# A two-layer hybrid decoder trunk in float32: the state's decay moved into keys and queries, two inverse roots queued later, and weight splits placed behind the first tile's transposed split

## The chip, the cores and the metric

The kernel runs on one core of a Trainium2 chip, in one launch. The metric is the time of one execution on the device in microseconds, as the median of several runs. The engines of the core are TensorE (PE, with its weight loads as PEld), VectorE (DVE), ScalarE (ACT), GpSimd (POOL) and SyncE (SP), which issues the transfers. Each engine works through its own queue of instructions in the order in which the program holds them; they wait for each other by semaphores.

## The reference

The input x is (1, 256, 1024) in float32. Two layers of three parts each follow: a half-step SwiGLU, a mixer, another half-step SwiGLU. Each part is normed on both sides.

```python
x = x + 0.5 * rmsnorm((silu(h @ w_gate) * (h @ w_up)) @ w_down, post_g)   # h = rmsnorm(x, pre_g)
x = x + rmsnorm(mixer(rmsnorm(x, pre_g)), post_g)
```

The mixer of layer 0 is a sparse attention beside a gated short convolution. The mixer of layer 1 is RWKV-7: for each of 16 heads a state of 64 by 64 runs over the 256 steps,

```python
def step(state, inp):
    r_t, w_t, k_t, v_t, kk_t, a_t = inp
    sa = jnp.einsum("bhij,bhj->bhi", state, -kk_t)
    state = (state * w_t[:, :, None, :] + sa[..., None] * (kk_t * a_t)[:, :, None, :]
             + v_t[..., None] * k_t[:, :, None, :])
    return state, jnp.einsum("bhij,bhj->bhi", state, r_t)
```

and its output is normed by head, given a bonus and a gate, and projected.

## The kernel before

Six stages run one after the other: `l0_ffn1`, `l0_mix`, `l0_ffn2`, `l1_ffn1`, `l1_mix`, `l1_ffn2`. The 256 rows of x are two tiles of 128 (`m` = 0 and 1). Every matmul with weights is made of three (`mm3`, lines 282 to 284): each operand is split into a high part that PE can take at its fast rate and a low remainder, and high by high, high by low and low by high are added up in PSUM. Weights come in transfers of up to 1 MB into one of four `raw` buffers; a piece of 1024 columns is split by `split_free`: ACT writes the high part (`L241`), DVE the remainder in one instruction or, for every `share`-th piece, POOL in two (`L246`).

**From one stage to the next.** The last part of a stage is `out_proj`: it finishes tile 0 first, then tile 1. `post_norm` takes the banks of a finished tile: ACT sums the squares (`L297`), ACT and POOL make the inverse root (`rstd`, `L290` and `L291`), DVE adds the result to x (`L356`). While PE works on tile 1, the next stage's `pre_norm` treats tile 0: squares, the product with the gain (`xg`, `L314`), the inverse root, and the scaling to `xn` (`L319`). `hT_split` has PE transpose `xn` (`L326`) and splits the result (`split`, ACT `L217`, DVE `L218`). PE's first matmuls of the next stage read both halves of it.

In the meantime the first weight pieces of the next stage are split too. `pre_norm` of tile 0 sets `self.held` to a list of instructions and `self.free` to 4. The first four pieces after it are free, and every later one is issued only after the instructions of that list (`split_u`). Before the change the list holds the latest square, product with the gain and inverse root.

Nothing here fixes the whole order by hand: a scheduler gives each engine its queue, under the data's order and these added constraints. So where an instruction stands has to be read from the built program.

**The RWKV chain.** The 256 steps are four chunks of 64 (`j` = 0 to 3). `kstep` prepares, for each of eight blocks of two heads (`c`), a tile `KR(c)` that holds for each chunk the scaled kappa and r side by side (columns 0 to 63 and 64 to 127), and `BK(c)` with the keys; `ff[:, c, j]` is the decay over chunk `j`. `gram` multiplies `BK` by `KR` (PE `L1145`). `chain(j)` then applies the state: `KR` times state into the banks `kb` (`L1338`), further terms (`L1342`), the scaled result `u` (DVE `L1344`), a small solve (`L1355`, copied by ACT in `L1356`), the chunk's contribution to the state into a bank `b` (`L1363`), the new state, and the output (`L1378`). For `j` = 1 and 2 the new state is decay times old state (POOL, `sf`) plus decay times `b` (DVE, `L1366` and `L1371`); for `j` = 0 there is no old state, and DVE multiplies `b` by the decay (`L1373`). `chunk_norm(j)` sums squares, makes an inverse root of 16 values for 64 rows (`L1403` to `L1408`, with ACT's square root `L1404` in between) and scales the output (`L1418`). `head_out(m)` applies gate and bonus (`L1428`, `L1429`) and has PE transpose the result for the last projection.

The string `TAIL` gives the order in which these generators are advanced (digits: `chain`; a to d: `chunk_norm(0)` to `(3)`, the first letter(s) sums, the next the root, then the scaling; p and q: `head_out`; o: the projection), and PE's instructions are kept in that order. `FILL` gives the order of work that fills the base solve ahead of it.

## Time and profile before

| | |
|---|---|
| time, median of 3 runs | 1160.28 us (1158.94 to 1164.31) |
| time of the profiled execution | 1160.69 us |
| its span, first to last instruction | 1159.0 us, mean granted TensorE clock 0.978 |
| busy: PE, DVE, ACT, POOL | 1093.6, 701.2, 601.0, 429.6 us (94, 61, 52, 37% of the span) |
| chain that ended last | 76% PE, 15% DVE, 4% issue, 3% ACT, 1% POOL |
| memory traffic | 185 MB read, 161 GB/s over the span |

The shares of busy time are means over stages. The 1.7 us between the time and the span lie around the first and the last instruction. Where a text names a time of day such as "at 197 us", it counts from the start of the span. A granted clock of 1.00 is PE's full rate.

### The profile page before, as it was taken

The numbers are of one execution on the slowest core, as the hardware profiler recorded it, in microseconds if no ns is written. First come the engines' busy times: TensorE is split into PE (matmuls) and PEld (weight loads), VectorE is DVE, ScalarE is ACT, GpSimd is POOL, SyncE is SP. The second block draws the span as 40 slices with busy tenths as digits, with TensorE's granted clock in tenths as the row PEclk, the third lists the DMA queues.
The fourth block names the chain that finished last, engine by engine and source line by source line (L and its number), as shares of the span: only waits on it lengthen the run. The fifth ranks groups of instructions, "written<-read, shape, count | busy, mean of one in ns | idle before, by whom it ended". The sixth has DMA issues, their size and how long they took to land.

```text
span 1159.0 us, 16840 instructions
## 1 busy us (share of the span) xinstructions
PE 1093.6 (94%) x6429; PEld 921.9 (80%) x6429; DVE 701.2 (61%) x1177; ACT 601.0 (52%) x1130; POOL 429.6 (37%) x390
## 2 busy tenths in 40 slices
...
GB/s 331 252 216 180 184 207 89 148 146 73 163 164 168 231 207 171 205 182 180 164 201 200 184 184 126 145 147 74 92 54 92 57 150 160 244 192 188 176 109 36
DMA packets 130749, 187.46 MB, mean 162 GB/s; under 512 B 6871, under 2 KB 101087, under 8 KB 130670
## 3 DMA queue, kind: packets, MB, share of 16 engines
...
HBM read 185.34 MB, written 1.05 MB: 161 GB/s over the span
## 4 chain that ended last, share of the span: by engine, by line
PE 76%; DVE 15%; issue 4%; ACT 3%; POOL 1%; DMA 0%; SPq 0%; DVEq 0%; POOLq 0%; ACTq 0%
PE mm L429 10%; PE fl L429 10%; PE fl L284 7%; PE fl L282 6%; PE fl L283 6%; PE fl L430 5%; PE mm L430 5%; PE mm L282 5%; PE mm L284 5%; PE mm L283 5%; DVE u L246 3%; PE tr L326 2%; PE fl L433 1%; PE mm L433 1%; DVE xn L1220 1%
## 5 line engine op out<-in xcount | busy, mean ns | idle before, releaser
L246 POOL TENSOR_TENSOR u<-raw,u 128x512 fp32r<-128x512 f32 x222 | 321.7, 1471 | 496.1 <-ACT u L241 490.4
L241 ACT ACTIVATE u<-raw 128x1024 fp32r<-128x1024 f32 x312 | 327.5, 1058 | 276.7 <-PE mm L283 78.5
L246 DVE TENSOR_TENSOR u<-raw,u 128x1024 fp32r<-128x1024 f32 x201 | 272.7, 1362 | 210.5 <-ACT u L241 210.2
L429 PE MATMUL mm<-b,u 128*128 128x512 f32 x504 | 181.3, 398 | 0.0
L429 PE MATMUL fl<-b,u 128*128 128x512 f32 x504 | 180.6, 397 | 0.0
L430 PE MATMUL fl<-b,u 128*128 128x256 f32 x504 | 141.5, 281 | 0.0
L430 PE MATMUL mm<-b,u 128*128 128x256 f32 x504 | 141.4, 281 | 0.0
L284 PE MATMUL fl<-u,b 128*128 128x512 f32 (+1 forms) x304 | 118.4, 390 | 3.5 <-DVE b L218 3.0
L282 PE MATMUL fl<-u,b 128*128 128x512 f32 (+1 forms) x304 | 118.7, 393 | 2.6 <-DVE u L800 1.3
L283 PE MATMUL fl<-u,b 128*128 128x512 f32 (+1 forms) x304 | 118.4, 389 | 1.5 <-DVE u L246 1.5
L282 PE MATMUL mm<-u,b 128*128 128x512 f32 (+1 forms) x296 | 114.7, 389 | 0.0
L283 PE MATMUL mm<-u,b 128*128 128x512 f32 (+1 forms) x296 | 113.0, 383 | 0.0
L284 PE MATMUL mm<-u,b 128*128 128x512 f32 (+1 forms) x296 | 112.5, 382 | 0.0
L429 PEld LDWEIGHTS mm<-b,u 128*128 128x128 f32 x504 | 94.8, 188 | 19.7
L429 PEld LDWEIGHTS fl<-b,u 128*128 128x128 f32 x504 | 94.9, 188 | 19.5
L430 PEld LDWEIGHTS mm<-b,u 128*128 128x128 f32 x504 | 95.2, 189 | 3.3
L430 PEld LDWEIGHTS fl<-b,u 128*128 128x128 f32 x504 | 95.2, 189 | 3.1
L284 PEld LDWEIGHTS fl<-u,b 128*128 128x128 f32 x304 | 57.8, 190 | 16.9 <-DVE b L218 4.3
L282 PEld LDWEIGHTS fl<-u,b 128*128 128x128 f32 x304 | 58.0, 191 | 15.1 <-ACT b L217 2.0
L283 PEld LDWEIGHTS fl<-u,b 128*128 128x128 f32 x304 | 58.0, 191 | 12.9 <-DVE u L246 1.7
L282 PEld LDWEIGHTS mm<-u,b 128*128 128x128 f32 (+1 forms) x296 | 55.8, 189 | 11.8 <-issue 0.7
L283 PEld LDWEIGHTS mm<-u,b 128*128 128x128 f32 (+1 forms) x296 | 55.9, 190 | 10.6
...
## 6 DMA issues: line engine op xcount, KB each, us to landing
...
```

The source lines that it names most:

```text
L241: self.nc.scalar.activation(hi, src, AF.Copy)
L246: (self.nc.gpsimd if pool else self.nc.vector).tensor_sub(lo[c], src[c], hi[c].bitcast(F32))
L282: mm(out, a[0], b[0], start=start, stop=False)
L283: mm(out, a[0], b[1], start=False, stop=False)
L284: mm(out, a[1], b[0], start=False, stop=stop)
L326: t = self.nc.tensor.transpose(pt[:, j * P:(j + 1) * P], src[:, j * P:(j + 1) * P], self.ident)
L429: mm(b2, w[k][0], x, start=k == 0, stop=False)
L430: mm(b2[:, 0], w[k][1], x[:, 0], start=False, stop=False)
L433: mm(b2, w[k][0], x, start=False, stop=True)
L1220: ins = [e.tensor_tensor(x, x, t, op=ALU.subtract) for e, x, _, _, t in act]
```

## The change

There are three parts.

1. **Decay.** New ACT copies (`decayed()`, 24 of 128 by 128) multiply chunk `j` of `KR(c)` by the decay of chunk `j` − 1, for `j` = 1 to 3. The state is kept without its last decay: for `j` = 1 and 2 DVE adds `b`, read from PSUM, to `sf`, and the four multiplications `L1366` are gone; `sf` uses the decay of chunk `j` − 1. For `j` = 0 the state is a plain copy of `b`, two quarters of it by DVE and two by ACT.
2. **TAIL.** The root of chunk 1 and that of chunk 2 are advanced later, and the transposed half of `head_out(0)` with them.
3. **Stage changes.** The list `held` of tile 0 now is the high and the low part of its transposed split and the inverse root (square, scaled x and inverse root where the stage takes its gain by columns), and none of the four free pieces goes to POOL. POOL's instructions for splits fall from 222 to 204, nine pieces; DVE's rise by nine.

```diff
-    FILL = "vvvz-vvtvvvbvvvhth-vvvvtthvtvtvv-h-vv-h-"
+    FILL = "vvvz-vvtvvvbvvvhthkvvvvtthvtvtvvkhkvvkh-"
-    TAIL = ("vvvgvz0xxvxx0A00gAggsB0eA000aAy1a1y1a1aa1yBy11b1bb2B22b2B2b222ocpocc33cc33p3d/3dooddodqooo"
+    TAIL = ("vvvgvz0xxvxx0A00gAggsB0eA000aAy1a1y1a1aa1yBy11b1b2B2b2b2B2b222ococ33cpcc33p3d/3dooddodqooo"
...
-                self.hT_split(self.pre_norm(m, g), hl, m)
+                hi, lo = self.hT_split(self.pre_norm(m, g), hl, m)
+                if m == 0:
+                    self.held[:2] = hi.ins, lo.ins
...
-        pool = self.share and self.nlo % self.share == 0
+        pool = self.share and self.nlo % self.share == 0 and self.free < 0
...
-                self.tail_of["xg"] = nc.vector.tensor_tensor(xg[:, sl], self.x[m][:, sl], g[:, sl], op=ALU.mult).ins
+                nc.vector.tensor_tensor(xg[:, sl], self.x[m][:, sl], g[:, sl], op=ALU.mult)
         r = self.rstd(ss)
+        for sl in self.HALF:
+            self.tail_of["xn"] = nc.vector.tensor_scalar(xn[:, sl], xg[:, sl], r, None, op0=ALU.mult).ins
         if m == 0 and g is not None:
-            self.held, self.free = list(self.tail_of.values()), 4
-        for sl in self.HALF:
-            nc.vector.tensor_scalar(xn[:, sl], xg[:, sl], r, None, op0=ALU.mult)
+            self.held, self.free = [self.tail_of[n] for n in ("sq", "xn", "pow")], 4
...
-            ffb = lambda ps, cs: ff[ps, cs, j:j + 1].to_broadcast([ps.stop - ps.start, cs.stop - cs.start, 64])
+            ffb = lambda ps, cs: ff[ps, cs, j - 1:j].to_broadcast([ps.stop - ps.start, cs.stop - cs.start, 64])
...
-                    if j:
-                        t = u[:, h * 512:h * 512 + 256].rearrange("p (c i) -> p c i", c=4)
-                        V.tensor_mul(t, b, ffb(slice(0, P), ch[h]))
...
-                            V.tensor_add(dst, sf[ps, ch[h]], t[ps])
+                            V.tensor_add(dst, b[ps], sf[ps, ch[h]])
+                        elif q:
+                            SC.activation(dst, b[ps], AF.Copy)
                         else:
-                            V.tensor_mul(dst, b[ps], ffb(ps, ch[h]))
+                            V.tensor_copy(dst, b[ps])
...
+        def decayed():
+
+            for c in range(NC):
+                for j in range(1, CH):
+                    SC.activation(KR(c)[:, j, :], KR(c)[:, j, :], AF.Copy, scale=ff[:, c, j - 1:j])
+                if c % 2:
+                    yield
```

Line numbers of the changed kernel are higher by 2 from line 216 on and by 3 from about line 353 on, up to `chain`: `L246` is `L248` there, `L291` is `L293`, `L326` is `L328`, `L356` is `L359`, `L1344` is `L1347`; in `chunk_norm` and `head_out` they are higher by 2 (`L1403` is `L1405`).

**Queues at the change into `l0_ffn2`.** POOL's queue there, before: the rows `L246` are the halves of weight pieces, `L291` the inverse roots, in order of tile 0's `post_norm` and `pre_norm` and the same two of tile 1.

```order
L246 TENSOR_TENSOR u<-raw,u 128x512 [waits PE_49,DMAHW3_49,Activation_49,Pool_49]
L246 TENSOR_TENSOR u<-raw,u 128x512
L246 TENSOR_TENSOR u<-raw,u 128x512 [waits DMAHW4_49,PE_49,Activation_49]
L246 TENSOR_TENSOR u<-raw,u 128x512
L291 TENSOR_TENSOR rstd_3124<-rstd,nhalf 128x1 [waits Activation_49]
L291 TENSOR_TENSOR rstd_3141<-rstd,nhalf 128x1 [waits Activation_49]
L246 TENSOR_TENSOR u<-raw,u 128x512 [waits DMAHW6_49,PE_49,Activation_49]
L246 TENSOR_TENSOR u<-raw,u 128x512
L291 TENSOR_TENSOR rstd_3220<-rstd,nhalf 128x1 [waits Activation_49]
```

POOL's queue at the same place after the change:

```order
L937 AFFINE_SELECT pk<-pk 64x64 [waits DVE_49,Pool_49]
L937 AFFINE_SELECT pk<-pk 64x64
L293 TENSOR_TENSOR rstd_3122<-rstd,nhalf 128x1 [waits Activation_49,Pool_49]
L293 TENSOR_TENSOR rstd_3139<-rstd,nhalf 128x1 [waits Activation_49]
L293 TENSOR_TENSOR rstd_3218<-rstd,nhalf 128x1 [waits Activation_49]
L248 TENSOR_TENSOR u<-raw,u 128x512 [waits DMAHW6_49,PE_49,Activation_49]
L248 TENSOR_TENSOR u<-raw,u 128x512
L293 TENSOR_TENSOR rstd_3235<-rstd,nhalf 128x1 [waits Activation_49]
L248 TENSOR_TENSOR u<-raw,u 128x512 [waits DVE_49,DMAHW0_49,PE_49,Activation_49]
```

The first two pieces have left POOL, and the first three inverse roots stand ahead of the splits. On DVE at the same place, before: `L314` is the product with the gain, `L319` the scaling, `L218` the low part of the transposed split.

```order
L314 TENSOR_TENSOR xn<-x_96,gain 128x512 [waits DVE_49] x2
L300 TENSOR_SCALAR sse<-ss 128x1 [waits Activation_49] x2
L353 TENSOR_TENSOR xn<-mm,gain 128x512
L246 TENSOR_TENSOR u<-raw,u 128x1024 [waits DMAHW5_49,PE_49,Activation_49]
L319 TENSOR_SCALAR xn<-xn,rstd_3141 128x512 [waits DVE_49,Pool_49]
L319 TENSOR_SCALAR xn<-xn,rstd_3141 128x512 [waits DVE_49]
L246 TENSOR_TENSOR u<-raw,u 128x1024 [waits PE_49,Activation_49]
L246 TENSOR_TENSOR u<-raw,u 128x1024 [waits DMAHW6_49,PE_49,Activation_49]
L218 TENSOR_TENSOR b_3018<-tr,b_3018 128x4x128 [waits Activation_49]
L218 TENSOR_TENSOR b_3019<-tr,b_3019 128x4x128 [waits Activation_49]
L246 TENSOR_TENSOR u<-raw,u 128x1024 [waits DMAHW7_49,PE_49,Activation_49]
```

And after:

```order
L248 TENSOR_TENSOR u<-raw,u 128x1024 [waits PE_49,Activation_49]
L356 TENSOR_TENSOR xn<-fl,gain 128x512 [waits Activation_49]
L359 SCALAR_TENSOR_TENSOR x_96<-xn,rstd_3122,x_96 128x512 [waits DVE_49,Pool_49]
L359 SCALAR_TENSOR_TENSOR x_96<-xn,rstd_3122,x_96 128x512 [waits DVE_49]
L316 TENSOR_TENSOR xn<-x_96,gain 128x512 [waits DVE_49] x2
L302 TENSOR_SCALAR sse<-ss 128x1 [waits Activation_49] x2
L356 TENSOR_TENSOR xn<-mm,gain 128x512
L319 TENSOR_SCALAR xn<-xn,rstd_3139 128x512 [waits DVE_49,Pool_49]
L319 TENSOR_SCALAR xn<-xn,rstd_3139 128x512 [waits DVE_49]
L220 TENSOR_TENSOR b_3016<-tr,b_3016 128x4x128 [waits Activation_49]
L220 TENSOR_TENSOR b_3017<-tr,b_3017 128x4x128 [waits Activation_49]
L248 TENSOR_TENSOR u<-raw,u 128x1024 [waits DMAHW5_49,Activation_49]
```

Between the product with the gain and the split's low part (`L220`) three weight pieces stood; none does now, the held pieces (`L248`) follow behind it, and more free ones stand ahead of the residual update (`L359`), of which one is shown.

**DVE in the state chain.** Around the root of chunk 1 and that of chunk 2, before (`L1344` is the first use of the banks `kb` of `j` = 2 and then of `j` = 3, `L1428` and `L1429` are `head_out(0)`):

```order
L1403 TENSOR_SCALAR var<-var 64x16 [waits DVE_49]
L1405 RECIPROCAL rs<-root 64x16 [waits Activation_49]
L1406 TENSOR_TENSOR root<-rs 64x16 [waits DVE_49]
L1407 SCALAR_TENSOR_TENSOR root<-root,var 64x16 [waits DVE_49]
L1408 SCALAR_TENSOR_TENSOR rs<-root,rs 64x16 [waits DVE_49]
L1344 SCALAR_TENSOR_TENSOR xn<-mm,pk 64x512 [waits PE_49] x2
L1418 TENSOR_TENSOR xn<-mm,rs 64x512 [waits DVE_49]
L1366 TENSOR_TENSOR xn<-tr,pk 128x256 [waits DVE_49,PE_49]
```

```order
L1371 TENSOR_TENSOR u<-xn 64x256 [waits DVE_49]
L1371 TENSOR_TENSOR u<-xn 64x256
L1428 TENSOR_TENSOR xn<-xn,u 128x512 x2
L1429 TENSOR_TENSOR xn<-xn,u 128x512 [waits DVE_49] x2
L1344 SCALAR_TENSOR_TENSOR xn<-mm,pk 64x512 [waits PE_49] x2
L1403 TENSOR_SCALAR var<-var 64x16 [waits Activation_49]
L1405 RECIPROCAL rs<-root 64x16 [waits Activation_49]
L1406 TENSOR_TENSOR root<-rs 64x16 [waits DVE_49]
```

After the change, the same two places:

```order
L1371 TENSOR_TENSOR u<-tr,xn 64x256
L1396 TENSOR_REDUCE var<-xn 64x8 [waits Activation_49] x2
L1347 SCALAR_TENSOR_TENSOR xn<-mm,pk 64x512 [waits PE_49] x2
L1405 TENSOR_SCALAR var<-var 64x16 [waits DVE_49]
L1407 RECIPROCAL rs<-root 64x16 [waits Activation_49]
L1408 TENSOR_TENSOR root<-rs 64x16 [waits DVE_49]
L1409 SCALAR_TENSOR_TENSOR root<-root,var 64x16 [waits DVE_49]
L1410 SCALAR_TENSOR_TENSOR rs<-root,rs 64x16 [waits DVE_49]
L1420 TENSOR_TENSOR xn<-mm,rs 64x512 [waits DVE_49]
L1371 TENSOR_TENSOR u<-tr,xn 64x256 [waits PE_49,Pool_49]
```

```order
L1371 TENSOR_TENSOR u<-tr,xn 64x256 [waits PE_49]
L1371 TENSOR_TENSOR u<-tr,xn 64x256
L1347 SCALAR_TENSOR_TENSOR xn<-mm,pk 64x512 [waits PE_49] x2
L1405 TENSOR_SCALAR var<-var 64x16 [waits Activation_49]
L1407 RECIPROCAL rs<-root 64x16 [waits Activation_49]
L1408 TENSOR_TENSOR root<-rs 64x16 [waits DVE_49]
L1409 SCALAR_TENSOR_TENSOR root<-root,var 64x16 [waits DVE_49]
L1410 SCALAR_TENSOR_TENSOR rs<-root,rs 64x16 [waits DVE_49]
L1430 TENSOR_TENSOR xn<-xn,u 128x512 x2
L1431 TENSOR_TENSOR xn<-xn,u 128x512 [waits DVE_49] x2
L1420 TENSOR_TENSOR xn<-mm,rs 64x512 x2
```

The root of chunk 1 has moved behind `L1347` of `j` = 2; at `j` = 3, `L1347` now stands ahead of the root of chunk 2 and of `head_out(0)`, and both stand ahead of the transposes that wait for the latter.

**ACT.** At `j` = 0, before: `L1238` is a copy for the second half of the solve's matrix, `L1477` the load of the table with the square root and a root that nothing reads, `L1398` the sums of squares of chunk 0.

```order
L1236 ACTIVATE xn<-u 32x1024 [waits Pool_49]
L1238 ACTIVATE b_7813<-u 32x32x32
L1477 ACT_TABLE_LOAD
L1477 ACTIVATE root<-pk 128x1
L976 ACTIVATE gain<-mm 128x512
L1398 ACTIVATE xn,var<-mm 64x64 [waits DVE_49,PE_49]
L1398 ACTIVATE xn,var<-mm 64x64 x7
```

And after, with the state's two quarters (`L1373`):

```order
L1241 ACTIVATE b_7829<-u 32x32x32
L1487 ACT_TABLE_LOAD
L1487 ACTIVATE root<-pk 128x1
L1373 ACTIVATE u<-tr 64x256 [waits DVE_49]
L979 ACTIVATE gain<-mm 128x512
L1400 ACTIVATE xn,var<-mm 64x64 [waits PE_49]
L1373 ACTIVATE u<-tr 64x256 [waits DVE_49]
L1400 ACTIVATE xn,var<-mm 64x64 x7
```

The first quarter stands behind the table load and the second behind the first of the sums. In the loop over the eight blocks, one pass of ACT before (`L1108` and `L1109` are the exponentials, `L1135` a head's sum split, `L1104` the tanh):

```order
L1135 ACTIVATE b_6836<-xn 128x256 [waits Activation_49]
L241 ACTIVATE u<-raw 128x1024 [waits DMAHW4_49]
L1108 ACTIVATE xn<-xn 128x256 [waits DVE_49]
L1104 ACTIVATE xn<-fl,pk 128x4x64 [waits DVE_49,PE_49]
L1104 ACTIVATE xn<-fl,pk 128x256 [waits PE_49]
L1109 ACTIVATE xn<-xn 128x260 [waits Activation_49]
```

After:

```order
L1138 ACTIVATE b_6828<-xn 128x256 [waits Activation_49]
L1447 ACTIVATE b_6452<-b_6452,pk 128x128 [waits PE_49] x2
L243 ACTIVATE u<-raw 128x1024 [waits DMAHW4_49]
L1447 ACTIVATE b_6452<-b_6452,pk 128x128 [waits PE_49]
L1111 ACTIVATE xn<-xn 128x256 [waits DVE_49]
L1107 ACTIVATE xn<-fl,pk 128x4x64 [waits DVE_49,PE_49]
L1107 ACTIVATE xn<-fl,pk 128x256 [waits PE_49]
```

Three copies (`L1447`) have come in, around the split of a weight piece and ahead of the exponential.

## Rows read from the trace of the kernel before

**Rows 1.** The page: busy time of PE with its share of the span, and of the costliest groups the one of DVE's halves of the weight splits (`L246`, one piece of 1024 columns each; columns: count, then busy us and mean ns of one, then DVE's idle time just before them and what ended most of it).

```profile
PE 1093.6 (94%) x6429; PEld 921.9 (80%) x6429; DVE 701.2 (61%) x1177; ACT 601.0 (52%) x1130; POOL 429.6 (37%) x390
...
L246 DVE TENSOR_TENSOR u<-raw,u 128x1024 fp32r<-128x1024 f32 x201 | 272.7, 1362 | 210.5 <-ACT u L241 210.2
```

**Rows 2.** Busy time of the engines in three stretches (start:end, length, then PE, PEld, DVE, ACT and POOL with their counts, the granted clock of PE as a share of full speed, the DMA share and GB/s).

```profile
347.00:350.00 3.00, 3.00 (x11) 2.39 (x9) 3.00 (x2) 2.59 (x5) 2.89 (x2) 0.50 0.05 9
965.00:968.00 3.00, 3.00 (x9) 2.34 (x8) 3.00 (x3) 2.23 (x5) 0.42 (x1) 0.50 0.49 134
782.00:837.00 55.00, 42.48 (x311) 30.77 (x310) 49.99 (x110) 35.68 (x91) 25.04 (x39) 1.00 0.21 70
```

**Rows 3.** PE at the stage changes. The first four lines are PE's timeline (start us, us, engine, line, operation, tiles, shapes, count, and in brackets the idle time before it and what ended it) at T1 and T2; the last four are the waits of PE (us in total, times, longest) between 530 and 543 us (T3) and between 953 and 966 us (T5).

```profile
198.60 1.09 PE L326 MATMUL tr<-ident,xn 128*128 128x128 f32 x8 [1.78 <-DVE xn L319]
202.46 0.50 PE L284 MATMUL fl<-u,b 128*128 128x512 f32 x1 [1.35 <-DVE b L218]
346.28 1.33 PE L326 MATMUL tr<-ident,xn 128*128 128x128 f32 x8 [4.06 <-DVE xn L319]
351.63 0.50 PE L284 MATMUL fl<-u,b 128*128 128x512 f32 x1 [1.09 <-DVE b L218]
...
PE tr L326 <- DVE xn L319: 1.7, 2, 0.9
PE fl L284 <- DVE b L218: 0.6, 1, 0.6
...
PE tr L326 <- DVE xn L319: 1.3, 1, 1.3
PE tr L326 <- DVE sse L300: 0.8, 1, 0.8
```

**Rows 4.** The timelines of POOL and ACT around T1 and T2: two POOL pairs of split halves (`L246`), one at T1 and one at T2, and the ACT instruction that hands over a root's input (`L290`), at T1 and at T2.

```profile
192.62 3.91 POOL L246 TENSOR_TENSOR u<-raw,u 128x512 fp32r<-128x512 f32 x2 [0.63 <-ACT u L241]
...
337.17 2.52 POOL L246 TENSOR_TENSOR u<-raw,u 128x512 fp32r<-128x512 f32 x2 [6.59 <-ACT u L241]
...
193.29 0.30 ACT L290 ACTIVATE rstd<-ss,sse 128x1 f32<-128x1 f32 x1 [0.75 <-DVE sse L300]
...
336.99 0.28 ACT L290 ACTIVATE rstd<-ss,sse 128x1 f32<-128x1 f32 x1
```

**Rows 5.** DVE's timeline around T1, T2 and T5: small splits of one stage's weights (`L218` on `u`), the residual update (`L356`), the product with the gain (`L314`) and two weight pieces (`L246`).

```profile
198.86 1.81 DVE L218 TENSOR_TENSOR u<-raw,u 128x768 fp32r<-128x768 f32 x4
...
340.25 1.41 DVE L356 SCALAR_TENSOR_TENSOR x<-xn,rstd,x 128x512 f32<-128x512 f32 x2 [3.38 <-POOL rstd L291]
341.58 1.29 DVE L314 TENSOR_TENSOR xn<-x,gain 128x512 f32<-128x512 f32 x2
...
346.45 4.53 DVE L246 TENSOR_TENSOR u<-raw,u 128x1024 fp32r<-128x1024 f32 x2
...
957.17 2.38 DVE L314 TENSOR_TENSOR xn<-x,gain 128x512 f32<-128x512 f32 x2
```

**Rows 6.** DVE's groups between 867 and 945 us, shapes kept apart (count, then busy us and mean ns of one, then idle time before them).

```profile
L1371 DVE TENSOR_TENSOR u<-xn 64x256 f32<-64x256 f32 x8 | 8.1, 1008 | 0.3
...
L1366 DVE TENSOR_TENSOR xn<-tr,pk 128x256 f32<-128x256 f32 x4 | 1.7, 424 | 2.9 <-PE tr L1363 2.8
```

**Rows 7.** PE's timeline in the state chain, from `j` = 0 to `j` = 3.

```profile
889.84 1.98 PE L1248 MATMUL tr<-xn,u 32*32 32x32 f32 x32
...
893.38 1.86 PE L1338 MATMUL mm<-u,b 128*128 128x128 f32 x7 [0.47 <-DVE pk L977]
...
908.33 1.16 PE L1338 MATMUL mm<-u,b 128*128 128x128 f32 x8 [0.59 <-DVE xn L1418]
910.28 1.16 PE L1338 MATMUL mm<-u,b 128*128 128x128 f32 x8 [0.79 <-DVE u L1371]
...
916.09 2.92 PE L1355 MATMUL tr<-xn,b 64*64 64x64 f32 x32 [2.64 <-DVE xn L1344]
...
926.57 1.16 PE L1338 MATMUL mm<-u,b 128*128 128x128 f32 x8 [1.34 <-DVE u L1371]
...
930.76 2.07 PE L1355 MATMUL tr<-xn,b 64*64 64x64 f32 x32 [1.03 <-DVE xn L1344]
```

**Rows 8.** DVE's timeline in the same stretch.

```profile
904.91 2.63 DVE L1371 TENSOR_TENSOR u<-xn 64x256 f32<-64x256 f32 x2
...
909.37 0.85 DVE L1371 TENSOR_TENSOR u<-xn 64x256 f32<-64x256 f32 x2
...
911.45 1.06 DVE L1403 TENSOR_SCALAR var<-var 64x16 f32<-64x16 f32 x1
...
915.25 1.28 DVE L1344 SCALAR_TENSOR_TENSOR xn<-mm,pk 64x512 f32<-64x512 f32 x2
...
926.54 1.29 DVE L1428 TENSOR_TENSOR xn<-xn,u 128x512 f32<-128x512 f32 x2
927.75 2.36 DVE L1429 TENSOR_TENSOR xn<-xn,u 128x512 f32<-128x512 f32 x2
```

**Rows 9.** POOL's timeline there: the state's decay `sf` of `j` = 2, and the pause before it.

```profile
910.30 2.18 POOL L1351 TENSOR_TENSOR xn<-u,pk 64x512 f32<-64x512 f32 x2 [3.04 <-DVE u L1371]
```

**Rows 10.** ACT's timeline at `j` = 0: the load of the table with the square root.

```profile
890.53 1.28 ACT L1477 ACT_TABLE_LOAD   x1
```

**Rows 11.** Of ACT's groups over the whole span, the scaled pass over a tile of 128 by 128.

```profile
L722 ACT ACTIVATE xn<-xn,nm 128x128 f32<-128x128 f32 x16 | 6.2, 388 | 2.8 <-DVE nm L720 2.8
```

9 lines of the change are left out of this document (5 added, 4 removed).

## The prediction

> **What bounds the kernel now.** I read the page first: TensorE (PE) is busy 1093.6 us, 94% of the span of 1159.0 [rows 1]. So a change is worth what it takes out of PE's idle 65 us, and I looked for that idle time where the diff acts: in the windows by stage, then in the waits and the timelines of PE, POOL, DVE and ACT around them.
>
> Three kinds of place matter. (a) The changes from one stage to the next (five: T1 at 197 us, T2 at 342, T3 at 535, T4 at 726, T5 at 962). PE stops there for the transposes (L326) of tile 0's normed x, which wait for the scaling L319, and once more for the low half of their split (L218): 1.78 and 1.35 us at T1, 4.06 and 1.09 at T2, 1.7 and 0.6 at T3, 1.3 and 0.8 at T5 [rows 3]; T4 has no gap. (b) The loop over the eight blocks of keys (782 to 837 us): DVE is busy 50.0 of 55 us, PE 42.5, ACT 35.7 [rows 2]. (c) The state chain (890 to 945 us), where PE waits for DVE.
>
> **The stage changes.** L319 needs the inverse root that POOL computes (L291). In before, POOL's queue has weight-split pairs (L246) ahead of it. At T1 ACT delivered the root's input at 193.59 us, but POOL was in a pair from 192.62 to 196.53. At T2 the first root waited behind a pair from 337.17 to 339.69 although its input was there at 337.27, 2.4 us lost [rows 4]. After the change POOL's roots stand ahead of the splits, as the order shows at T2. Worked from rows:
> - T1: root at about 193 us, a little earlier still since DVE's work ahead of it is not stretched beside POOL's pair, L319 done near 195.8, before PE runs dry at 196.8, so 1.78 goes. Behind L319 stand the six small splits and the other tile's product, some 3.7 us (1.81 for four of the splits [rows 5]), so the low half lands at 200.2 and PE resumes there instead of 202.46. Saved: 2.3.
> - T2: without the last L241 ahead of it the root's input comes near 336.1, the root at 336.8; the residual update (1.41), the gain product (1.29) [rows 5], the sums and the second root follow, L319 at 340.8 to 341.6. PE has work until 342.2. Then the low half follows L319 directly, where two weight pieces of together 4.53 us stood before. I take 4.9 of the 5.15.
> - T3: the same two waits, 2.3 in all; I take 2.25.
> - T5: the root was not late behind POOL's pair there, but its input was: the residual update and the gain product ran beside the pair, the product for 2.38 instead of 1.29 us [rows 5]. Both back to T2's length would give 2.1; I take 1.9.
> - T4: one more weight piece (1.36 [rows 1]) now stands ahead of the residual update in a place that had no gap: a loss between 0 and 1.36; I take 0.5.
>
> Sum 10.85. The price is nine weight pieces that move from POOL to DVE, 9 × 1.36 = 12 us of DVE. I cost them at nothing, because they go where DVE idled: 3.38 us ahead of the residual update at T2 [rows 5]. Where that cover is missing they delay the pieces that PE needs next; that is the first rival.
>
> **The clock.** Behind T2's gap PE worked without a pause from 347 to 350 us at a granted clock of 0.50, and behind T5's from 965 to 968 [rows 2]: 1.2 instead of 2.4 GHz, so each 3 us of work would take 1.5 at the full clock. If the gaps shrink to a few tenths the clock may stay up. Between 0 and 3.0 I take 1.5.
>
> **The decay.** Eight additions L1371 read two SBUF tiles and take 1.01 us in the mean, four multiplications L1366 from PSUM 0.42 [rows 6]. After the change the four are gone and the addition reads PSUM and SBUF. Its price is not in the trace; its bounds are 0.42 (the operation from PSUM over the same 256 columns) and 1.01. I take 0.42, because L1366 keeps 0.42 in the same stretch, with POOL as busy, and L1371 does not. The old form itself shows the cause: two of them took 2.63 us beside POOL's work and two took 0.85 [rows 8] in POOL's pause of 3.04 us before 910.30 [rows 9]. The Trainium skill (GPSIMD Engine Reference, section 1) says that POOL shares its SBUF interfaces with VectorE and contends with its instructions of two SBUF inputs; by it the price is 0.42 as well, and by the other reading, that POOL's work slows whatever reads SBUF, 1.01. The trace decides for the first, since the multiplication reads SBUF too, but one tile of it. At 1.01 the tail would come out 1.2 us longer.
>
> **The chain's tail, in order of time [rows 7, 8, 10].**
> - j=0: half of the state is now copied by ACT, whose queue has a table load ahead of it, to 891.81 us, and a small root. The copy ends near 892.45 (0.42 for a pass of 256 columns, as on DVE). The matmuls L1248 reuse the bank that it reads, so they start then instead of at 889.84. This loses 2.6, less a gap of 0.47 that it covers: 2.1.
> - j=1: the waits of 0.59 and 0.79 go, the first for a product queued behind the state's additions: gain 1.4, of which I keep 1.2 for a PSUM bank that DVE frees later.
> - j=2: the inverse root of chunk 1 (from 911.45 to L1344's start at 915.25) stood ahead of L1344, on which PE waited 2.64. Now L1344 is first: 2.4.
> - j=3: the wait of 1.34 goes, and that of 1.03 mostly. But the root of chunk 2 and head_out(0) now stand between L1344 and the transposes L326 that wait for head_out. The root is 3 us or more (3.8 for chunk 1), head_out up to the first half 1.29 and half of 2.36, in all 5.5 or more; PE's own work in between, 2.07, covers so much of it. I take 3.2 for what PE then lacks. Net −0.9.
>
> Together: −2.1 + 1.2 + 2.4 − 0.9 = 0.6; I take 0.4, since every term is a little uncertain, with −4 and +4 as ends (all new waits as long as their whole queue, or none exposed).
>
> **The prescaling.** 24 ACT copies of 128x128 are new. The nearest row is a scaled pass of that size at 0.388 us [rows 11]: up to 9.3 us. They stand in the loop over keys, two ahead of a weight split and one ahead of the exponential. ACT has 19 us free there, but DVE, the bound of the stretch, waits for ACT's results. Ends: nothing, and 9.3. Tracing one pass, most successors have 2 to 4 us of slack, and one split in a pass is late by some 0.2: I take 8 × 0.2 = 1.6.
>
> **Sum.** 1160.69 − 10.85 − 1.5 − 0.4 + 1.6 = 1149.5; the profiled run's own time, 1.7 us over its span, is 0.4 above the median of three, within their spread, so 1149.5 stands for the median. A measurement of this kernel tells about 0.5% (5.8 us) from no change.
>
> **Rivals.**
> 1. Stage starts starve. Four held pieces now follow the transposed split on DVE, 1.36 us each. PE's next pieces are due when its 24 matmuls into the first bank (5.5 us) are done. If they come one piece late at each of five changes: 5 × 1.36 = 6.8 back, 1156.3. Against it: traced as above, T2's first held piece is ready near 346 us and due at 349.5. 0.15.
> 2. The ACT copies are wholly exposed, since DVE is 91% busy there: 9.3 instead of 1.6, 1157. For it: the exponential feeds DVE's products. 0.09.
> 3. Slower than before, one mechanism: the four held pieces at each of five stage changes are all exposed on DVE's queue ahead of what PE needs, 5 × 4 × 1.36 = 27 us: 1176.6. It makes the kernel slower from the point where 9 of the 20 are exposed (12 us against a gain of 11). For it: 12 us more on DVE near these places. Against: the 5.5 us of matmuls at each that cover four pieces of 1.36. 0.05.
> 4. The decay part does not do what it says: L1371 stays at 1.01 because POOL's work, not the operand, slows it, and the new waits at j=0 and j=3 stay: 2 to 4 us more, 1153. 0.14.
> 5. The moved pieces read two SBUF tiles, so DVE runs them beside POOL's next pair at 2.27 us rather than 1.36, as the two of 4.53 at T2 did [rows 5]. Nine cost 8 us more, half of it exposed: 1153.5. For it: POOL still has pairs just behind the roots. 0.09. The Trainium skill (SBUF — State Buffer, section "SBUF: two separate sides") would call this an exclusive lock on the shared port, held for a whole instruction by whichever engine starts first.
>
> The forecast holds 0.48, within 1145 to 1153.
>
> **Chances.** Faster by over 0.5% means under 1154.5. Forecast and rival 4 lie there, and half of rivals 1 and 5: 0.62 + 0.12 = 0.74. Same: the rest of 1, 5 and 2: 0.20. Slower: 0.06, rival 3 with a little of 2. The range reaches to rivals 1 and 2 above, and below to the whole clock gain with the tail's upper end (1149.5 − 1.5 − 4).
>
> **What would show it.** Right: POOL's root at T1 ends near 193.5 us and at T2 before 337.5; no PE gap over 0.5 us for L319; L1371 near 0.42 us; a wait of PE near 890 us for ACT's copy, and one of 3 us before the transposes of head_out(0). Wrong: PE gaps on L248's pieces behind a stage change; the stretch of 55 us longer by over 3.

## The result, and the profile after

The changed kernel takes 1154.41 us in the median of 17 runs (1149.69 to 1163.54), the kernel before 1164.31 in as many runs beside it (1158.01 to 1171.43). The ratio is 0.9922, with a 95% interval of 0.99 to 0.9944: faster by 0.78%, some 9 us.

The time lies inside the range of the prediction, from 1144.0 (1149.5 − 1.5 − 4) up to rivals 1 and 2 (1156.3 and 1157), but above the 1145 to 1153 that it gave the forecast itself. That forecast started from 1160.69 for the kernel before, which took 1164.31 beside the change; the ratio times 1160.69 is 1151.6, inside that band.

The forecast change was 11.2 us (1160.69 to 1149.5); the interval holds 6.5 to 11.6, so 11.2 lies near its edge. So the total was met. The sum behind it was not met in all its terms, and the range holds rivals 1, 2, 4 and 5 as well, so the time alone tells nothing of the mechanism.

The page after the change, in the lines that answer to [rows 1], and the chain that ended last:

```profile
PE 1100.3 (95%) x6429; PEld 929.4 (80%) x6429; DVE 688.3 (59%) x1180; ACT 606.1 (52%) x1156; POOL 408.0 (35%) x372
...
PE 76%; DVE 11%; issue 4%; ACT 4%; POOL 3%; DMA 1%; SPq 0%; DVEq 0%; POOLq 0%; ACTq 0%
...
L248 DVE TENSOR_TENSOR u<-raw,u 128x1024 fp32r<-128x1024 f32 x210 | 279.5, 1338 | 217.5 <-ACT u L243 216.9
```

DVE's pieces have gone from 201 to 210, as the diff says, and one takes 1338 ns where it took 1362. POOL is busy 22 us less. PE is busy longer (1100.3 for 1093.6) with the same instructions: the profiled run's granted clock was 0.969, that of before 0.978. Its time was 1158.8 us, above its median, and it is read here by its stretches, not by its total.

**The stage changes.** PE's timeline at T2 and T5, in the first rows of the transposes of tile 0 and of tile 1 (the last bracket: idle time before, and what ended it):

```profile
345.38 1.06 PE L328 MATMUL tr<-ident,xn 128*128 128x128 f32 x8 [0.17 <-DVE xn L319]
359.60 1.06 PE L328 MATMUL tr<-ident,xn 128*128 128x128 f32 x8 [1.39 <-DVE xn L319]
...
957.59 1.04 PE L328 MATMUL tr<-ident,xn 128*128 128x128 f32 x8
...
973.58 1.94 PE L328 MATMUL tr<-ident,xn 128*128 128x128 f32 x8 [3.26 <-DVE xn L319]
```

At tile 0 the waits of [rows 3] are gone: 4.06 has become 0.17 at T2, and T5 has none. The wait for the low half is gone at T2 as well; at T1 0.71 of its 1.35 us are left. But tile 1, which had no such wait before, now has one. PE's waits from 525 to 570 us (T3; us in total, times, longest) show the same:

```profile
PE tr L328 <- DVE xn L319: 1.4, 1, 1.4
PE fl L284 <- ACT b L219: 0.2, 1, 0.2
```

Added up over T1, T2, T3 and T5, PE's waits for the norm and its split fall from 13.7 to 8.9 us; 6.9 of the 8.9 are new waits for tile 1's norm (0.8, 1.4, 1.4 and 3.3), and 0.7 is a new one for its split at T1.

Why tile 1 is late at T5 is read from the queues. POOL's timeline there, with tile 1's two roots:

```profile
961.86 3.53 POOL L248 TENSOR_TENSOR u<-raw,u 128x512 fp32r<-128x512 f32 x2 [5.72 <-ACT u L243]
965.35 1.53 POOL L293 TENSOR_TENSOR rstd<-rstd,nhalf 128x1 f32<-128x1 f32 x1
966.85 2.98 POOL L248 TENSOR_TENSOR u<-raw,u 128x512 fp32r<-128x512 f32 x2
...
972.36 0.55 POOL L293 TENSOR_TENSOR rstd<-rstd,nhalf 128x1 f32<-128x1 f32 x1 [2.53 <-ACT rstd L292]
```

ACT's, with the instruction that hands over the first root's input (L292) and a table load ahead of the second square sum:

```profile
961.66 0.30 ACT L292 ACTIVATE rstd<-ss,sse 128x1 f32<-128x1 f32 x1
...
969.46 1.28 ACT L467 ACT_TABLE_LOAD   x1
```

And DVE's, two held weight pieces, tile 1's residual update (L359) and its scaling (L319):

```profile
962.94 3.53 DVE L248 TENSOR_TENSOR u<-raw,u 128x1024 fp32r<-128x1024 f32 x2 [0.82 <-ACT u L243]
966.91 3.47 DVE L359 SCALAR_TENSOR_TENSOR x<-xn,rstd,x 128x512 f32<-128x512 f32 x2 [0.44 <-POOL rstd L293]
972.95 0.88 DVE L319 TENSOR_SCALAR xn<-xn,rstd 128x512 f32<-128x512 f32 x2 [1.30 <-POOL rstd L293]
```

The root's input is there at 961.96, but POOL began a pair at 961.86, and the root starts 3.4 us late. POOL's next pair runs beside the residual update, which takes 3.47 us instead of 1.41 [rows 5]. This is what the prediction read at tile 0 in [rows 4], one tile later: the pieces that were moved behind tile 0's split now stand ahead of, and beside, tile 1's norm.

The Trainium skill (SBUF — State Buffer, section "SBUF: two separate sides") calls the port that VectorE and GpSimd share an exclusive lock, held for a whole instruction, where a VectorE instruction reads two SBUF tiles, as L359 does. By it, L359 and the pair, 1.41 and 2.52 us when undisturbed [rows 4, 5], would need 3.93 one after the other, an estimate; they took 3.53, from 966.85 to 970.38. The trace agrees that each delays the other, but not that they wholly exclude each other: some 0.4 us of the work overlaps.

**The clock at these places.** Granted clock behind T2's and T5's changes, in windows with the columns of [rows 2]:

```profile
345.00:352.00 7.00, 6.83 (x34) 5.52 (x34) 5.36 (x8) 5.63 (x9) 2.15 (x2) 1.00 0.16 48
966.00:980.00 14.00, 10.74 (x41) 8.56 (x40) 8.77 (x12) 5.71 (x11) 4.38 (x4) 0.76 0.48 151
```

T2 now runs at full clock, where before it fell to 0.50 from 347 to 350 [rows 2]. Behind the new wait at T5 it falls instead, to 0.76 over 14 us.

**The state chain.** PE's timeline at `j` = 0, `j` = 1 and at the transposes of `head_out(0)`:

```profile
887.94 1.26 PE L1251 MATMUL tr<-xn,u 32*32 32x32 f32 x19 [2.56 <-ACT u L1373]
...
903.60 1.17 PE L1258 MATMUL tr<-b,xn 32*32 32x32 f32 x32 [1.90 <-DVE u L1371]
...
927.21 1.09 PE L328 MATMUL tr<-ident,xn 128*128 128x128 f32 x4 [3.20 <-DVE xn L1431]
```

The group that answers to [rows 6], and ACT's copies, between 865 and 945 us, shapes apart, with the columns of those rows:

```profile
L1371 DVE TENSOR_TENSOR u<-tr,xn 64x256 f32<-64x256 f32 x8 | 3.4, 422 | 1.3 <-PE tr L1366 1.1
...
L1373 ACT ACTIVATE u<-tr 64x256 f32<-64x256 f32 x2 | 0.7, 370 | 0.0
```

PE waits 2.56 us for ACT's copy and 3.20 for `head_out(0)`, both where the prediction put them. The 1.90 at `j` = 1 was not foreseen, and not every kernel with ACT's copy has it (see `j0_dve`): on DVE an instruction of chunk 0's root (L1410, 0.86 us) stands between the first addition L1371, at 901.69, and the second, at 903.03. The waits of 1.34 and 2.64 of [rows 7] are gone. The additions take 0.422 us, against 1.008 before [rows 6].

**The ledger.** PE's time, cut at the same instructions in each kernel (worked out from PE's timelines; a stage change is the stretch from the last matmul ahead of tile 0's transposes to the third set of transposes behind them; in us):

| kernel | T1 | T2 | T3 | T5 | keys | chain to `head_out(0)` | from there to T5 | `l0_mix` |
|---|---|---|---|---|---|---|---|---|
| before | 31.8 | 36.5 | 32.3 | 34.6 | 124.3 | 65.5 | 28.9 | 113.6 |
| after | 30.9 | 31.4 | 31.1 | 36.6 | 123.9 | 63.6 | 30.5 | 117.5 |
| `stage_only` | 30.9 | 31.4 | 31.1 | 36.8 | 123.0 | 64.4 | 30.7 | 113.8 |
| `decay_tail` | 31.8 | 36.5 | 32.3 | 32.7 | 126.7 | 65.9 | 30.4 | 114.2 |
| `held_only` | 32.4 | 33.6 | 31.2 | 36.9 | 125.0 | 64.0 | 30.7 | 111.2 |
| `free_only` | 30.3 | 31.5 | 29.6 | 31.2 | 123.8 | 65.8 | 32.0 | 115.1 |
| `free_stage` | 30.3 | 31.5 | 29.6 | 35.3 | 123.1 | 65.8 | 31.7 | 112.3 |
| `pool_late` | 30.6 | 31.5 | 30.1 | 34.3 | 123.2 | 64.7 | 30.8 | 117.7 |
| `j0_dve` | 30.9 | 31.4 | 31.1 | 36.5 | 123.8 | 60.4 | 30.5 | 117.5 |
| `head_mid` | 30.9 | 31.4 | 31.0 | 35.3 | 125.2 | 64.8 | 34.0 | 109.2 |
| `free_j0_head` | 30.3 | 31.5 | 29.6 | 31.6 | 124.0 | 59.1 | 31.4 | 107.9 |

From before to after the stage changes give 5.2 us, the keys 0.4 and the tail 0.3 (1.9 won, 1.6 lost again). T4 and the rest agree to 0.1. These times hold what the clock costs, too: T2's 36.5 us have 3 us at 0.50 in them [rows 2], and T5's 36.6 have 7 us at 0.51, from 973 to 980. The 1.6 lost behind `head_out(0)` are of that kind. Windows over that stretch, before and after (columns of [rows 2]):

```profile
933.00:963.00 30.00, 26.04 (x142) 20.75 (x141) 28.58 (x37) 18.51 (x31) 15.64 (x12) 1.00 0.46 150
```

```profile
927.00:958.00 31.00, 28.45 (x145) 23.52 (x146) 27.05 (x37) 16.14 (x28) 14.73 (x10) 0.92 0.46 143
```

`stage_only` and `free_stage`, whose edits leave the tail as before, take 30.7 and 31.7 us there, at 0.91 and 0.90. `l0_mix`, which the change leaves as it was, is 3.9 us longer in this profile, and differs by 8 us between after and `head_mid`, whose instructions are the same there: this is the clock (last section). For that reason the verdicts below go by the ratios, and the ledger says only where; a microsecond or two in it can be the clock.

### The profile page after: what moved, and what is told of

It reads as the page before. It is cut to its first block, busy times and chain, and to the rows that moved or that the text cites. A ratio compares the mean times of both kernels' runs of the same rounds, so it can differ in the third digit from the quotient of the medians.

```text
span 1157.0 us, 16840 instructions
## 1 busy us (share of the span) xinstructions
PE 1100.3 (95%) x6429; PEld 929.4 (80%) x6429; DVE 688.3 (59%) x1180; ACT 606.1 (52%) x1156; POOL 408.0 (35%) x372
## 4 chain that ended last, share of the span: by engine, by line
PE 76%; DVE 11%; issue 4%; ACT 4%; POOL 3%; DMA 1%; SPq 0%; DVEq 0%; POOLq 0%; ACTq 0%
PE mm L432 10%; PE fl L432 10%; PE fl L284 6%; PE fl L286 6%; PE fl L285 6%; PE mm L433 5%; PE fl L433 5%; PE mm L284 5%; PE mm L286 5%; PE mm L285 5%; DVE u L248 3%; PE tr L328 2%; PE mm L436 1%; PE fl L436 1%; DVE xn L1223 1%
## 5 line engine op out<-in xcount | busy, mean ns | idle before, releaser
L248 POOL TENSOR_TENSOR u<-raw,u 128x512 fp32r<-128x512 f32 x204 | 293.6, 1461 | 481.9 <-ACT u L243 475.6
L248 DVE TENSOR_TENSOR u<-raw,u 128x1024 fp32r<-128x1024 f32 x210 | 279.5, 1338 | 217.5 <-ACT u L243 216.9
L293 POOL TENSOR_TENSOR rstd<-rstd,nhalf 128x1 f32<-128x1 f32 x24 | 22.7, 945 | 140.7 <-ACT rstd L292 140.7
L285 PEld LDWEIGHTS fl<-u,b 128*128 128x128 f32 x304 | 58.1, 191 | 12.8 <-DVE u L248 1.7
L284 PEld LDWEIGHTS mm<-u,b 128*128 128x128 f32 (+1 forms) x296 | 55.4, 188 | 11.8 <-issue 0.8
```

What stands on the lines that cost most here:

```text
L248: (self.nc.gpsimd if pool else self.nc.vector).tensor_sub(lo[c], src[c], hi[c].bitcast(F32))
L284: mm(out, a[0], b[0], start=start, stop=False)
L285: mm(out, a[0], b[1], start=False, stop=False)
L293: self.tail_of["pow"] = nc.gpsimd.tensor_tensor(r2, r, self.nhalf, op=ALU.pow).ins
```

## The experiments

The first theory: the gain is POOL's. The free pieces no longer go to POOL, so the roots at a stage change no longer wait behind a pair. Its rival: the gain is DVE's, because the held pieces stand behind the transposed split. Of the other parts the theory says that they cancel each other.

The table gives the median, the ratio to the kernel before with its 95% interval, and the difference at equal clock. This last column comes from a straight line through time against granted clock, with one slope for all kernels, over 187 runs (one run at a clock of 0.917 left out); the slope is −8.1 us for each +0.01, and the scatter about it 1.6 us. Where a wait less keeps the clock up, this column leaves that share of the gain out.

| kernel | median us | ratio | at equal clock, us |
|---|---|---|---|
| after | 1154.41 | 0.9922 [0.99, 0.9944] | −8.3 |
| `stage_only` | 1152.8 | 0.9929 [0.9903, 0.9955] | −8.7 |
| `decay_tail` | 1163.0 | 1.0012 [0.9983, 1.004] | −1.2 |
| `decay_only` | 1165.08 | 1.0041 [1.0008, 1.0073] | +0.7 |
| `tail_only` | 1162.92 | 1.0015 [0.9985, 1.0046] | +1.1 |
| `held_only` | 1164.42 | 1.0015 [0.9986, 1.0045] | −1.3 |
| `free_only` | 1152.51 | 0.9902 [0.9869, 0.9935] | −11.3 |
| `free_stage` | 1150.2 | 0.9886 [0.984, 0.9931] | −8.8 |
| `pool_late` | 1148.47 | 0.9879 [0.984, 0.9918] | −12.8 |
| `j0_dve` | 1151.36 | 0.9897 [0.9857, 0.9937] | −10.7 |
| `head_mid` | 1155.6 | 0.9938 [0.9906, 0.997] | −7.4 |
| `free_j0_head` | 1140.12 | 0.9807 [0.9765, 0.9849] | −15.0 |
| `free_j0_head_late` | 1145.79 | 0.9862 [0.9814, 0.991] | −11.8 |

**`stage_only`**: the kernel before with the third part of the change alone. Of its edit the two lines that count:

```diff
+                    self.held[:2] = hi.ins, lo.ins
-        pool = self.share and self.nlo % self.share == 0
+        pool = self.share and self.nlo % self.share == 0 and self.free < 0
```

> The change of the stages alone (held list, no free piece on POOL); decay and TAIL as before. Theory A, read from the two traces between fixed matmuls: the wait for tile 0 goes, but the split pieces now stand ahead of tile 1's norm, and PE waits there (0.85, 1.39, 1.40 and 3.26 us at T1, T2, T3 and T5 in the trace of the changed kernel); what is left is 5 us, so 3 to 8 us less than before. Theory B, the sum of the prediction: 10.85 us and 1.5 of clock, so 11 to 13 less. Rival C: the gain of the whole change comes from decay and TAIL, and this is within 2 us of before.

Measured 0.9929, 8.2 us less: the upper end of theory A's 3 to 8, short of theory B's 11 to 13, and the whole gain of the change, within the intervals. Rival C is out.

**`decay_tail`**: the first two parts alone, without the lines above.

```diff
-    TAIL = ("vvvgvz0xxvxx0A00gAggsB0eA000aAy1a1y1a1aa1yBy11b1bb2B22b2B2b222ocpocc33cc33p3d/3dooddodqooo"
+    TAIL = ("vvvgvz0xxvxx0A00gAggsB0eA000aAy1a1y1a1aa1yBy11b1b2B2b2b2B2b222ococ33cpcc33p3d/3dooddodqooo"
-                            V.tensor_add(dst, sf[ps, ch[h]], t[ps])
+                            V.tensor_add(dst, b[ps], sf[ps, ch[h]])
```

> Decay and TAIL together, stage changes as before. Theory A and the prediction's terms agree here: the tail gains 0.4 to 2 us and the loop over keys loses 0 to 1.6, so within 2 us of before. Rival C: 5 us or more less than before. PE's wait for ACT's copy at j = 0 (2.6 us) and before the transposes of head_out(0) (3.2 us) are both in the trace.

Measured 1.0012, no difference, as the theory and the prediction's terms expected. PE's waits between 885 and 950 us in it:

```profile
PE tr L326 <- DVE xn L1428: 3.2, 1, 3.2
PE tr L1248 <- ACT u L1370: 2.6, 1, 2.6
```

They are the two new waits. That they take just what the cheaper additions and the moved roots give is read from the sum and not shown singly.

**`decay_only`**: the kernel before with the decay part, `TAIL` as before.

```diff
-                            V.tensor_add(dst, sf[ps, ch[h]], t[ps])
+                            V.tensor_add(dst, b[ps], sf[ps, ch[h]])
+                        elif q:
+                            SC.activation(dst, b[ps], AF.Copy)
```

> The decay alone, TAIL and stage changes as before. By the prediction's terms: the wait of PE at j = 0 costs 2.1, the waits for the state (0.79, 1.34) go, but the roots still stand ahead of the first use of the banks, so 0 to 2 us more than before with the ACT copies of the loop over keys. Rival: these copies are hidden and the shorter additions alone give 3 us or more.

Measured 1.0041, a loss by 0.1 to 0.7%, some 5 us where 0 to 2 were expected; at equal clock little of it is left (0.7 us). The shorter additions alone do not give 3 us. PE's waits from 885 to 960 us:

```profile
PE tr L1355 <- DVE xn L1344: 3.4, 1, 3.4
PE tr L1248 <- ACT u L1370: 2.6, 1, 2.6
PE tr L1255 <- DVE u L1368: 1.9, 1, 1.9
```

The 3.4 us come at `j` = 3, where without the new `TAIL` L1344 stands behind `head_out(0)`. DVE's timeline there, from the window of 918 to 946 us (L1427 and L1428 are `head_out(0)`):

```profile
932.39 3.38 DVE L1427 TENSOR_TENSOR xn<-xn,u 128x512 f32<-128x512 f32 x2
935.70 3.42 DVE L1428 TENSOR_TENSOR xn<-xn,u 128x512 f32<-128x512 f32 x2
939.15 1.28 DVE L1344 SCALAR_TENSOR_TENSOR xn<-mm,pk 64x512 f32<-64x512 f32 x2
```

The wait of 2.64 at `j` = 2 is gone in this profile, although the root of chunk 1 still stands ahead of L1344 there. The 1.9 at `j` = 1 is here without the new `TAIL`, so it does not need it.

**`tail_only`**: the kernel before with the new `TAIL` alone.

```diff
-    TAIL = ("vvvgvz0xxvxx0A00gAggsB0eA000aAy1a1y1a1aa1yBy11b1bb2B22b2B2b222ocpocc33cc33p3d/3dooddodqooo"
+    TAIL = ("vvvgvz0xxvxx0A00gAggsB0eA000aAy1a1y1a1aa1yBy11b1b2B2b2b2B2b222ococ33cpcc33p3d/3dooddodqooo"
```

> TAIL alone, decay and stage changes as before. By the prediction's terms: the wait of 2.64 us at j = 2 goes, and the wait before the transposes of head_out(0) comes, 3 us; the net lies between 2 us less and 1 us more than before.

Measured 1.0015. The new order gains nothing by itself either: the 2.64 at `j` = 2 is gone, but PE now waits 3.0 us (2.9 of it in one wait) before L1338 for the additions L1371, which are still long, and 1.8 before the transposes of `head_out(0)`, where 3 were expected.

**`held_only`**: the changed kernel, but free pieces may go to POOL again.

```diff
-        pool = self.share and self.nlo % self.share == 0 and self.free < 0
+        pool = self.share and self.nlo % self.share == 0
```

> The changed kernel with its new held list, but POOL takes every share-th piece again, the free ones too. If the order of POOL's queue (roots behind free pairs) is what cost T2 its 4.06 us, T2's segment is 34 to 36.5 us instead of 31.4 and the kernel 3 to 6 us slower than the changed one (ratio to before 0.995 or more). If the held list (no weight piece ahead of the split's low part) is what counts, T2 is 31 to 33 us and the ratio 0.992 to 0.994.

Measured 1.0015: without the condition the gain is gone. POOL's timeline at T2:

```profile
335.51 2.52 POOL L248 TENSOR_TENSOR u<-raw,u 128x512 fp32r<-128x512 f32 x2 [6.56 <-ACT u L243]
337.99 0.56 POOL L293 TENSOR_TENSOR rstd<-rstd,nhalf 128x1 f32<-128x1 f32 x1
```

The pair is ahead of the root again, and PE's wait at tile 0 of T2 is 2.4 us. So the theory stands against its rival: without the condition, the held list is worth nothing that can be measured in the total. Against before it gains 2.9 us at T2 and 1.1 at T3 in the ledger and loses 0.6 at T1 and 2.3 at T5. Two numbers were missed: T2's 33.6 is just below the 34 to 36.5 expected, and the loss against the changed kernel is 7 us at equal clock, where 3 to 6 were expected.

**`free_only`**: the changed kernel with the list as before it, so that the condition on POOL is all that is left of the third part.

```diff
-                if m == 0:
-                    self.held[:2] = hi.ins, lo.ins
-            self.held, self.free = [self.tail_of[n] for n in ("sq", "xn", "pow")], 4
+            self.held, self.free = [self.tail_of[n] for n in ("sq", "xg", "pow")], 4
```

> The changed kernel with the old held list (square, product with the gain, root), and no free piece on POOL. If POOL's queue is what counts, T2's segment is 31 to 33 us and the gap of 4.06 us is gone while the 1.09 us for the split's low part stays: ratio to before 0.991 to 0.995. If the held list counts, T2 is 34 us or more. T5: with the old list fewer pieces stand ahead of tile 1's norm, so its segment is shorter than 36.7 if the held pieces cause the new wait.

Measured 0.9902, and 3 us better than after at equal clock: the held list costs. DVE takes as many pieces here as in after (210), so it is not their number. T5 falls from 36.6 to 31.2 us in the ledger and T3 from 31.1 to 29.6. POOL's and DVE's rows of tile 1 at T5, of two timelines:

```profile
961.04 2.81 POOL L246 TENSOR_TENSOR u<-raw,u 128x512 fp32r<-128x512 f32 x2 [0.68 <-ACT u L241]
963.82 0.54 POOL L291 TENSOR_TENSOR rstd<-rstd,nhalf 128x1 f32<-128x1 f32 x1
```

```profile
964.39 1.41 DVE L357 SCALAR_TENSOR_TENSOR x<-xn,rstd,x 128x512 f32<-128x512 f32 x2 [1.75 <-POOL rstd L291]
```

The residual update has its 1.41 us again, with no pair beside it, and PE has no wait for tile 1. At tile 0 it waits 1.3 us for the scaling at T2 (0.17 in after) and 0.3 for the low half, of which 1.09 was expected to stay; for the low half it waits 1.4 at T1 and 0.4 at T5.

**`free_stage`**: the kernel before with the condition alone, nothing of the decay, `TAIL` or the list.

```diff
-        pool = self.share and self.nlo % self.share == 0
+        pool = self.share and self.nlo % self.share == 0 and self.free < 0
```

> The kernel before with one condition added: none of the four free weight pieces goes to POOL (held list, decay and TAIL as before). Theory (this condition makes the whole gain, the new held list costs at T3 and T5, decay and TAIL give nothing): segments T1, T2, T3, T5 near 30.3, 31.5, 29.6 and 31.2 us as in the version with the old held list, against 31.8, 36.5, 32.3 and 34.6 before; 11 us less than before, a ratio of 0.990. Rival (decay and TAIL, useless alone, help here): 0.993 or more.

Measured 0.9886. This one condition is as good as the whole change (0.9922), or a little better. But T5 here is 35.3 us, where 31.2 was expected from the kernel with the other two parts beside it: PE waits 2.12 and 0.78 us for tile 0's scaling. The other two parts shorten T5 in `decay_tail` too (32.7 for 34.6), while `decay_only` (34.6) and `tail_only` (34.8) do not. So the rival is right in this one place; why was not tried.

**`pool_late`**: the changed kernel, where the first four held pieces stay off POOL too.

```diff
-        pool = self.share and self.nlo % self.share == 0 and self.free < 0
+        pool = self.share and self.nlo % self.share == 0 and self.free < -4
```

> The changed kernel, but POOL takes none of the first eight weight pieces of a stage instead of the first four, so that none of its pairs stands ahead of or beside tile 1's norm. Between fixed matmuls (from the end of a stage's last matmuls ahead of the first transposes to the third set of transposes) the changed kernel took 30.9, 31.4, 31.1 and 36.7 us at T1, T2, T3 and T5. Theory A (POOL's pairs ahead of and beside tile 1's norm cause the new wait): T5 falls by 2 to 3.3 us, T2 and T3 by about 1.4 each, T1 by less, 4 to 6 us less than the changed kernel in all, a ratio to before near 0.987. Rival (DVE's own held pieces cause it, and there are more of them now): no segment shorter by over 0.5 us, ratio 0.991 or more.

Measured 0.9879, 4.5 us better than after at equal clock. T5's wait at tile 1 falls from 3.26 to 1.96 and T3's from 1.40 to 0.5: POOL's pair was part of the cause. At T5 the residual update takes 1.41 us again, but two held pieces stand behind it on DVE, the second of them beside POOL's next pair:

```profile
966.76 2.31 DVE L248 TENSOR_TENSOR u<-raw,u 128x1024 fp32r<-128x1024 f32 x1
```

```profile
966.23 3.99 POOL L248 TENSOR_TENSOR u<-raw,u 128x512 fp32r<-128x512 f32 x2 [2.57 <-ACT u L243]
```

So the rest is DVE's held pieces, and how much of it they would cost without that pair is not shown. T1's waits for tile 1 become one of 1.70, and T2 gets one of 1.19 at tile 0. In the ledger the four stage changes win 3.5 us against the changed kernel, where 4 to 6 were expected.

**`j0_dve`**: the changed kernel, the state of `j` = 0 copied by DVE alone.

```diff
-                        elif q:
-                            SC.activation(dst, b[ps], AF.Copy)
```

> The changed kernel with all four quarters of the state copied by DVE at j = 0. The wait of PE for ACT's copy (2.56 us, near 885) goes. Theory: PE gets there 2 to 2.6 us earlier and the kernel is 2 us faster than the changed one (ratio to before 0.990 to 0.991). Rival: the time is given back at the next wait, since DVE's results set the rest of the chain: within 0.5 us of the changed kernel, with the wait of 1.90 us at L1258 longer by as much.

Measured 0.9897, 2.4 us better than after at equal clock; the chain up to `head_out(0)` is 3.2 us shorter (63.6 to 60.4), everything else in the ledger the same. PE's waits there, from 880 to 925 us:

```profile
PE tr L328 <- DVE xn L1429: 3.2, 1, 3.2
PE mm L1341 <- DVE pk L980: 0.5, 1, 0.5
```

Both the 2.56 and the 1.90 are gone. But the 1.90 does not hang on ACT's copy alone: after, `held_only`, `pool_late` and `decay_only` have both waits, `decay_tail`, `free_only` and `head_mid` have the 2.56 and no 1.90. Windows from the first place to the second, of after and of `decay_tail`:

```profile
888.00:904.00 16.00, 14.11 (x205) 13.44 (x206) 9.32 (x16) 6.21 (x38) 5.64 (x5) 0.80 0.01 2
```

```profile
897.00:913.00 16.00, 16.00 (x190) 15.31 (x188) 8.50 (x16) 5.25 (x37) 5.55 (x5) 0.62 0.01 2
```

The four with the wait have a granted clock of 0.79 or 0.80 there, the three without it 0.62 to 0.65. PE, slower, works on where it otherwise waits, and the stretch is about as long either way: 15.7 to 16.0 us with the wait, 16.3 without; in before and in `j0_dve`, without ACT's copy, it is 14.2 and 14.4.

**`head_mid`**: the changed kernel with the root of chunk 2 behind `head_out(0)` instead of ahead of it.

```diff
-    TAIL = ("vvvgvz0xxvxx0A00gAggsB0eA000aAy1a1y1a1aa1yBy11b1b2B2b2b2B2b222ococ33cpcc33p3d/3dooddodqooo"
+    TAIL = ("vvvgvz0xxvxx0A00gAggsB0eA000aAy1a1y1a1aa1yBy11b1b2B2b2b2B2b222ococ33pccc33p3d/3dooddodqooo"
```

> The changed kernel with one letter of TAIL moved: head_out(0) is advanced behind the first use of the banks of j = 3 but ahead of the inverse root of chunk 2. Theory (the root of chunk 2 on DVE makes the 3.20 us that PE lacks before the transposes of head_out(0)): the gap falls to 0.5 us or less and the kernel is 1 to 3 us faster than the changed one, 0.990 to before. Rival: the root and the scaling of chunk 2 come later and PE waits for them behind, the segment to the next stage grows by as much, and the time stays at 0.992.

Measured 0.9938, no better than after. The wait for `head_out(0)` falls from 3.20 to 1.7, not to 0.5 or less, and PE waits 0.7 us behind it for the low half (L220), which stands on DVE behind the scaling of chunk 2. The stretch there grows from 30.5 to 34.0 us, but most of that is the clock, 0.86 for 0.92. So the rival's mechanism is there, with 0.7 us, and the total agrees with it.

**`free_j0_head`**: `free_only`, `j0_dve` and `head_mid` in one; **`free_j0_head_late`**: the same with the held pieces off POOL. Against the changed kernel, in the lines that count:

```diff
-            self.held, self.free = [self.tail_of[n] for n in ("sq", "xn", "pow")], 4
+            self.held, self.free = [self.tail_of[n] for n in ("sq", "xg", "pow")], 4
-                        elif q:
-                            SC.activation(dst, b[ps], AF.Copy)
...
-        pool = self.share and self.nlo % self.share == 0 and self.free < 0
+        pool = self.share and self.nlo % self.share == 0 and self.free < -4
```

The last two lines are in the second kernel alone; `TAIL` is that of `head_mid` in both.

> The changed kernel with the old held list, all of the state's copies at j = 0 by DVE, and head_out(0) ahead of the root of chunk 2. If the three corrections add up (old held list 3.5 us at equal clock, j = 0 3.0, head_out 1 to 2), it is 7 to 9 us faster than the changed kernel, a ratio to before of 0.984 to 0.986. If they share a bound, 0.988 or more.

> The last version, and POOL takes none of the first eight pieces of a stage. If POOL's pairs ahead of tile 1's root still cost with the old held list (a gap of 1.26 us at T2), T2 falls from 31.5 to about 30.5 us and the kernel by 1 to 2 more, a ratio to before of 0.982 to 0.985. Rival: DVE, with two more pieces per stage, now delays the norm: no faster, or a microsecond slower.

The first is the fastest kernel of the study: 1140.12 us, 0.9807 [0.9765, 0.9849] of before, and faster than after as well, by 14 us in the medians and 6.7 at equal clock, where 7 to 9 were expected. The span with the granted clock, and then a window in `l0_mix`:

```profile
core 0: 1136.7 us, clock 0.985
```

```profile
210.00:320.00 110.00, 105.33 (x798) 97.73 (x798) 77.92 (x216) 54.47 (x129) 41.95 (x37) 1.00 0.39 132
```

Its clock is above that of the others (0.983 in the mean of its six runs, 0.974 before), and at equal clock 15.0 of its 20 us are left. The single gains at equal clock would add up to some 12.8 (`free_only` 11.3, `j0_dve` 2.4 more, `head_mid` 0.9 less). Whether its clock is higher because fewer waits are left, or by chance, is open. Keeping the held pieces off POOL on top of that, which helped the changed kernel, harms here, as its rival said: 1145.79, with a new PE wait for DVE at T3 (1.15), longer ones at T5 (1.52 for 0.82) and at T2 (2.18 for 1.26), and T2 at 33.6 us, where 30.5 was expected. With the list as before, DVE is then what is late.

## Why the prediction was right, and where its sum was not

- **T1, predicted 2.3, measured 0.9.** The scaling is done in time, as worked out (DVE's L319 from 194.78 to 195.66; 195.8 was forecast), and PE resumes at 199.73, earlier than the 200.2 forecast. The root itself ended at 194.75, not 193.5: it took 2.21 us beside DVE's work, which harmed nothing. That is 2.7 earlier than before [rows 3], and tile 1's new waits, 1.5 in all, take more than half of it back.
- **T2, predicted 4.9, measured 5.1.** Right at tile 0, in its cause as well: `held_only` gives 2.2 of it back (33.6 for 31.4) by putting one pair ahead of the root, and `free_only`, with the list as before, keeps 5.0. But 5.1 meets 4.9 by luck. PE's waits there fall by 3.6 only (5.4 to 1.8), since tile 1 now waits 1.39; the other 1.5 is the 3 us at half clock that are gone, which the prediction had booked under the clock.
- **T3, predicted 2.25, measured 1.2; T5, predicted 1.9, measured −2.0.** The step that failed is the same at T1, T3 and T5. The nine moved pieces were costed at nothing "because they go where DVE idled", and that was traced up to tile 0's split. What stands next, tile 1's norm, was not traced. The waits there, 6.9 us, are more than the 5.65 by which the sum of 10.85 came out too high (5.2 in the ledger). `free_only`, which moves the same nine pieces and has no such wait, shows that they come from the held list, that is from where the pieces stand. One reading was wrong, too: the 0.8 at T5 is a second wait before the transposes, as its row says [rows 3], not one for the low half. Rival 1 was near it, but put the wait on the weight pieces that PE needs next; it is the norm that is late, not a piece.
- **T4, predicted −0.5**: unchanged.
- **The clock, predicted 1.5**: not realised in the sum. At T2 it stays up, as forecast, and at T5 it falls for longer behind the new wait. The mean granted clock is 0.974 over all runs of either kernel.
- **L1371, predicted 0.42**: 0.422. Rival 4's price of 1.01 is out. Its other half, that the new waits stay, is what `decay_tail` shows; the forecast had both in its sum.
- **The tail, predicted +0.4, +0.3 in the two profiles**: not told, since the 1.6 that is lost behind `head_out(0)` in that sum goes with the clock there. `j` = 0 was right (2.6 forecast, 2.56 in the trace; `j0_dve` gives 2.4 to 3.2 back) and so was the end of the wait at `j` = 2. At `j` = 1 a gain of 1.2 was forecast, and in this profile there is a wait of 1.90. At `j` = 3 3.2 and 3.20 agree in part by luck: the root of chunk 2 took 2.4 us on DVE where 3 or more was taken, `head_out(0)` up to its first half 1.9 where 2.5 was, and PE's own work covered 1.3 and not 2.07.
- **The prescaling, predicted −1.6**: not contradicted. The keys' stretch is 0.4 shorter, but the stage changes shorten it by 1.3 by themselves (`stage_only` 123.0, before 124.3). Between kernels that differ by the prescaling it is 0.7 to 2.4 longer (`free_only` and `free_stage`, after and `stage_only`, `decay_tail` and before). A copy takes 0.396 us, close to the row it was taken from [rows 11]. Rival 2, with 9.3, is out.
- **Rival 3** did not come: PE waits for no piece at the stage changes. **Rival 5** came in part: DVE's pieces take 1338 ns in the mean, not more, but at T5 two of them took 3.53 us beside POOL's pair, and the contention falls on tile 1's residual update as well. Of the signs on record, "no PE gap over 0.5 us for L319" fails, at tile 1.

By parts: `stage_only` measures −8.2 us (−0.71%) where 12.35 was forecast with the clock, `decay_tail` +1.4 (not told from nothing) where +1.2 was. The ledger's 5.2 for the stage changes is less than the 8 or so of the ratios. The ledger rests on one profile of each kernel, and that of before ran at 0.978, where the mean of its runs is 0.974, which is worth some 3 us by the slope. Some 1.3 us also lie over the keys, where the stage changes were given no term.
